# Up-projection products of 512 columns over both parts of the input, and the gate multiply on VectorE

## The chip, the cores and the metric

The kernel runs on one core of one Trainium2 chip. The metric is the device time in microseconds (us) of one execution. A core has five engines with queues of their own: TensorE (PE in the profile, its weight loads PEld), VectorE (DVE), ScalarE (ACT), GpSimd (POOL) and SyncE (SP, which here issues DMAs). They wait for each other by semaphores. TensorE writes its products into PSUM, eight banks of 512 float32 columns on 128 partitions; the other tiles lie in SBUF.

## The reference

A trunk of two transformer layers on 256 tokens of width 1024. Layer 0 has block-sparse attention, which at this length is plain causal attention, layer 1 has sliding-window attention with sinks. After each attention stands the channel mixer that the change touches:

```
def conv_ffn(h, w_up, conv_w, conv_b, w_down):
    S_ = h.shape[1]
    u = h @ w_up                                         # 1024 -> 2 * 2816
    up = jnp.pad(u, ((0, 0), (CONV_W - 1, 0), (0, 0)))
    u = conv_b + sum(conv_w[j] * up[:, j:j + S_] for j in range(CONV_W))
    gate, val = jnp.split(u, 2, axis=-1)
    return (jax.nn.silu(gate) * val) @ w_down

x = x + conv_ffn(rmsnorm(x, ffn_norm[l]), w_up[l], conv_w[l], conv_b[l], w_down[l])
```

All inputs and outputs are float32.

## The kernel before

**Split products.** Each float32 operand is split into a high part, rounded to the TensorE format float32r, and a low part, the remainder. A product is the sum of three: high by high, high by low and low by high. ScalarE rounds (`hi_part`, L177), VectorE subtracts (`lo_part`, L185).

**Weights.** All weights come as 90 units of 128 x 2048, 1 MB each. `fetch` (L166) issues the DMA on SP's queue into three raw buffers. `prepare(i)` splits a unit in two to eight pieces; its last step fetches unit i + 3. The high and the low parts have four buffers each. `used(i)` is called when the products of unit i have been issued, and lets unit i + 4 be prepared.

**Order of the work.** The program keeps a clock of its own: `tick` adds a planned time for each product issued on TensorE, and steps put off with `chain(key, (delay, step), ...)` are issued when the clock passes their due time. `require(key)` issues what is left of a chain at once. In the feed-forward part the scheduler of the framework may still move instructions within an engine's queue; each engine then runs its queue in order.

**The up-projection.** Per layer there are NF = 22 units; unit i holds for eight chunks c of the input the 128 gate columns (j = 0) and the 128 value columns (j = 1). The weights are the stationary operand, the 256 tokens the moving one. `mm` runs over j, then over the chunks: three products of 256 columns each (L683 high by high, L684 high weights by low input, L685 low weights by high input), 48 a unit. Gate and value land in the two halves of one PSUM bank. Units 0 to 3 (`i < n_raw`) read the input `hT` before its normalisation factor is known, and the factor is applied to their result; units 4 to 21 read `hS`, the scaled input, which `scale_x` splits into four pairs of chunks.

**After a unit, `post`.** ScalarE computes the last tap of the convolution with its bias (`tap2`, L718), VectorE adds the two others for gate and value (`taps`, L722 and L724), ScalarE applies SiLU (L728), GpSimd multiplies gate and value (L732), ScalarE rounds the result (L736), VectorE subtracts (L737). In units 4 to 21 `tap2` and `taps` read the PSUM bank itself. PSUM tags: "acc" has four banks, "t" and "u" two each; units 4 to 21 take one bank of "t" and "u" in turn.

**The down-projection, `Down`.** 11 weight units, each with two halves of 128 rows, two blocks of 128 tokens and products of 512 columns (L588, L589, L593), into the four "acc" banks. It needs the results of `post` for two up-projection units per weight unit.

The functions around the change:

Of the kernel before, what the change touches and what calls it, by code (L numbers as in the profile page):

```python
# [10 lines left out]
AF = mybir.ActivationFunctionType  # L11
ALU = mybir.AluOpType
AX = mybir.AxisListType

P = 128
D = 1024
S = 256
NB = S // P
KC = D // P
# [7 lines left out]
NF = DFF // P  # L27
# [32 lines left out]
def trunk(ctx: ExitStack, tc, x, xw, pos, cpk, fin, sinks, w, out):  # L60
    nc = tc.nc
# [8 lines left out]
    def nm(s):  # L70
        uid[0] += 1
        return f"{s}_{uid[0]}"
# [5 lines left out]
    def spaced(pool, n, dt, tag, name, bufs):  # L78
        return pool.tile([P, n + ROUND], dt, tag=tag, name=name, bufs=bufs)[:, SKIP:SKIP + n]

    def quad(dt=F32R, name="q"):
        return spaced(qd, 4 * S, dt, "q", nm(name), 15).rearrange("p (c t) -> p c t", c=4)

    def mid():
        return wk.tile([P, 512], F32, tag="m2", name=nm("m2"), bufs=6)

    def row3(n=3 * P):
        return wk.tile([P, 3 * P + 8], F32, tag="m3", name=nm("m3"), bufs=8)[:, 4:4 + n]
# [7 lines left out]
    def bank(tag):  # L96
        return ps.tile([P, 512], F32, tag=tag, name=nm(tag), bufs=4 if tag == "acc" else 2)

    def f(ap):
        return ap.bitcast(F32)  # L100
# [7 lines left out]
    def turns(ap):  # L108

        return ap.rearrange("p (a t) -> p t a", a=2)  # L110

    def pairs(ap):
        return ap.rearrange("p (t a) -> p t a", a=2)
# [8 lines left out]
    def run_item(item):  # L122
        put_off.remove(item)
        was, busy[0] = busy[0], True
        item[2]()
        busy[0] = was

    def tick(ns):
        clock[0] += ns
        while put_off and not busy[0]:  # L130
            item = min(put_off, key=lambda t: t[0])
            if item[0] > clock[0]:
                return
            run_item(item)

    def chain(key, *steps, urgent=0):

        def run(k):
            if urgent:
                with tc.high_priority(offset=urgent):  # L140
                    steps[k][1]()
            else:
                steps[k][1]()
            if k + 1 < len(steps):
                put_off.append((clock[0] + steps[k + 1][0], key, lambda: run(k + 1)))
        put_off.append((clock[0] + steps[0][0], key, lambda: run(0)))

    def require(*key):

        while True:  # L150
            mine = [t for t in put_off if t[1] == key]
            if not mine:
                return
            run_item(min(mine, key=lambda t: t[0]))


    wq = {}
# [55 lines left out]
    def used(i):  # L213

        prepare(i + 4)

    def need(i):
        require("w", i)
# [48 lines left out]
    for b in range(NB):  # L267
        t = one.tile([P, NH, HD], F32, name=f"v{b}")
# [12 lines left out]
    def new_hT():  # L281

        return [(quad(), quad()) for _ in range(2)]
# [71 lines left out]
    def hx(hT, c):  # L355
        hi, lo = hT[c // 4]
        return hi[:, c % 4], lo[:, c % 4]
# [306 lines left out]
    def ffn(layer, u_up, u_dn, hT, y, rb, after, tail=None):  # L664
        parts = []

        n_raw = 4
        hS = new_hT()

        def mm(i, up, cs_):  # L670
            need(u_up + i)
            hi, lo = wq[u_up + i]
            for j in range(2):
                o = up[j]
                for c in cs_:
                    if i < n_raw:
                        for b in range(NB):
                            require("x", b, c // 4)
                    else:
                        require("y", c // 2)  # L680
                    s_ = slice((2 * c + j) * P, (2 * c + j + 1) * P)
                    xh, xl = (turns(t) for t in hx(hT if i < n_raw else hS, c))
                    nc.tensor.matmul(pairs(o), hi[:, s_], xh, start=(c == 0), stop=False)  # L683
                    nc.tensor.matmul(pairs(o), hi[:, s_], xl, start=False, stop=False)  # L684
                    nc.tensor.matmul(pairs(o), lo[:, s_], xh, start=False, stop=(c == KC - 1))  # L685
                    tick(3 * 256 / 2.4)

        def scale_x(m):

            c = slice(2 * (m % 2), 2 * (m % 2) + 2)  # L690
            y_, hi, lo = (t[:, c] for t in (y[m // 2], *hS[m // 2]))

            def times():
                for b in range(NB):
                    require("rb", b)
                y4 = y_.rearrange("p c (a t) -> p c a t", a=2)
                r4 = rb.rearrange("p (t a) -> p a t", a=2).unsqueeze(1).to_broadcast([P, 2, 2, P])
                nc.vector.tensor_tensor(out=y4, in0=y4, in1=r4, op=ALU.mult)

            chain(("y", m), (2000.0 + 1000.0 * m, times), (700.0, lambda: nc.scalar.activation(hi, y_, AF.Copy)),  # L700
                  (600.0, lambda: nc.vector.tensor_tensor(out=lo, in0=y_, in1=f(hi), op=ALU.subtract)))

        def post(i, up, pq):
            hi, lo = pq[:, 2 * (i % 2)], pq[:, 2 * (i % 2) + 1]
            t = [row3(S) for _ in range(2)]
            gs, h = row3(S), row3(S)
            w0, w1, w2, bb = ([cp[:, CW + (layer * 2 * NF + j * NF + i) * 4 + k:][:, :1] for j in range(2)] for k in range(4))
            us = [mid()[:, :S] for _ in range(2)] if i < n_raw else up

            def scale():  # L710
                for b in range(NB):
                    require("rb", b)
                for j in range(2):
                    nc.vector.tensor_tensor(out=us[j], in0=up[j], in1=rb, op=ALU.mult)

            def tap2():
                for j in range(2):
                    nc.scalar.activation(t[j], us[j], AF.Identity, scale=w2[j], bias=bb[j])  # L718

            def taps():  # L720
                for j in range(2):
                    nc.vector.scalar_tensor_tensor(out=t[j][:, 1:], in0=us[j][:, :S - 1], scalar=w1[j], in1=t[j][:, 1:],  # L722
                                                   op0=ALU.mult, op1=ALU.add)
                    nc.vector.scalar_tensor_tensor(out=t[j][:, 2:], in0=us[j][:, :S - 2], scalar=w0[j], in1=t[j][:, 2:],  # L724
                                                   op0=ALU.mult, op1=ALU.add)

            def gate():
                nc.scalar.activation(gs, t[0], AF.Silu)  # L728
                if layer and i == NF - 1:

                    nc.scalar.activation(warm, gs[:, :1], AF.Sqrt, scale=0.0)
                nc.gpsimd.tensor_tensor(out=h, in0=gs, in1=t[1], op=ALU.mult)  # L732

            steps = [(200.0, scale), (700.0, tap2)] if i < n_raw else [(200.0, tap2)]
            chain(("p", i), *steps, (400.0, taps), (1600.0, gate),
                  (3400.0, lambda: nc.scalar.activation(hi, h, AF.Copy)),  # L736
                  (450.0, lambda: nc.vector.tensor_tensor(out=lo, in0=h, in1=f(hi), op=ALU.subtract)))  # L737
            parts.append((hi, lo))

        pq = quad()  # L740
        ups = [[bank(t)[:, :S] for _ in range(2)] for t in ("u", "acc")]
        for cs_ in (range(4), range(4, KC)):
            for i in range(2):
                mm(i, ups[i], cs_)
        for i in range(2):
            used(u_up + i)
            post(i, ups[i], pq)
        for m in range(4):
            scale_x(m)
        for i in range(2, NF):  # L750
            if i % 2 == 0:
                pq = quad()
            up = bank("acc" if i < 4 else "t" if i % 2 else "u")
            mm(i, [up[:, :S], up[:, S:]], range(KC))
            used(u_up + i)
            post(i, [up[:, :S], up[:, S:]], pq)

        def wait(i):
            require("p", 2 * i)
            require("p", 2 * i + 1)  # L760

        if tail is not None:
            nc.sync.dma_start(fin_t, fin.partition_broadcast(P))
        dn = Down(u_dn, NF // 2, parts, wait, tail is not None)
        for _ in dn.units(0, NF // 2 - 2):
            pass
        dn.finish(NF // 2 - 2, after, tail)
# [20 lines left out]
    hT = new_hT()  # L788
# [200 lines left out]
    hT = new_hT()  # L989
    y = [quad(F32, "y") for _ in range(2)]  # L990
# [13 lines left out]
    def after_f0(b, n):  # L1004
# [3 lines left out]
        raw_feats(b, n, xT_h, ("x", b, n))  # L1008

    ffn(0, U_UP0, U_DN0, hT, y, rb, after_f0)  # L1010


# [60 lines left out]
    hT = new_hT()  # L1073
    y = [quad(F32, "y") for _ in range(2)]
# [152 lines left out]
```

## Time and profile before

| | |
|---|---|
| time, median of 3 runs | 551.17 us (550.32 to 552.12) |
| profiled execution: time | 551.24 us |
| profiled execution: span from first to last instruction | 549.3 us |
| TensorE clock granted, mean | 0.998 |
| up-projection of layer 0, units 4 to 21 | about 136 to 233 us of the span |
| up-projection of layer 1, units 4 to 21 | about 389 to 486 us |
| GpSimd's 44 multiplies (L732) | 69.6 us busy, 1581 ns each on average |

In the rows below, a group reads: line, engine, operation, written tile <- read tiles, shapes, count, then busy time in us, mean ns of one, and idle time of the engine in front of them. Tile names: `wr` raw weights, `wh` and `wl` their high and low parts, `q` parts of activations, `m` intermediate rows in SBUF, `cp` the convolution's constants, and `acc`, `t`, `u` banks of PSUM.

A row of the busy time by windows reads: window, its length, then for each engine the busy time and the count of instructions, the granted clock, the DMA share and GB/s.

### The profile page before, as it was taken

How to read it: one execution, taken by the hardware profiler on the slowest of the kernel's cores; microseconds unless marked ns; L12 is line 12 of the kernel's file. 1: busy time of each engine (PE TensorE's matmuls, PEld its weight loads, DVE VectorE, ACT ScalarE, POOL GpSimd, SP SyncE). 2: the span in 40 equal slices, each digit the busy share in tenths (PEclk: the TensorE clock that was granted, in tenths of full speed). 3: DMA queues.
4: the chain of work that ended last, by engine and by line, in shares of the span. 5: the costliest groups of instructions: out<-in, count | busy, mean ns of one | idle time of the engine just before them, and what ended most of it. 6: DMA issues, size and time to landing. Idle time of an engine off the chain costs nothing.

```text
span 549.3 us, 9981 instructions
## 1 busy us (share of the span) xinstructions
PE 540.9 (98%) x3762; PEld 497.0 (90%) x3762; DVE 423.8 (77%) x901; ACT 373.3 (68%) x735; POOL 114.2 (21%) x155
## 2 busy tenths in 40 slices
PE   9999999999999999999999999999999999999995
PEld 7888888899999999988888887889999999998884
DVE  6798777589898888874468999878898898884514
ACT  6789778579577777754368888777657777683313
POOL 7312001011423332230000120102432332320003
PEclk9999999999999999999999999999999999999999
DMA  8975444432466556666552644242375656666201
GB/s 293 402 281 187 155 153 155 154 135 97 158 226 231 211 202 208 226 230 220 177 216 87 221 153 154 83 148 82 150 245 206 197 199 229 237 225 231 113 0 76
DMA packets 15311, 100.98 MB, mean 184 GB/s; under 512 B 1952, under 2 KB 2080, under 8 KB 3744
## 3 DMA queue, kind: packets, MB, share of 16 engines
q1 hardware_dynamic: 14976, 100.09, 50.5%
q8 instruction: 29, 0.48, 0.3%
q10 hardware_dynamic: 288, 0.26, 0.1%
q14 instruction: 18, 0.15, 0.1%
HBM read 99.30 MB, written 1.05 MB: 183 GB/s over the span
## 4 chain that ended last, share of the span: by engine, by line
PE 91%; ACT 3%; DMA 2%; DVE 2%; POOL 1%; issue 0%; ACTq 0%
PE acc L588 9%; PE acc L593 9%; PE acc L589 9%; PE u L683 7%; PE u L684 7%; PE u L685 6%; PE t L683 6%; PE t L684 6%; PE t L685 6%; PE acc L367 4%; PE acc L366 4%; PE acc L368 4%; PE acc L683 2%; PE acc L685 2%; PE acc L684 2%; PE t L538 2%
## 5 line engine op out<-in xcount | busy, mean ns | idle before, releaser
L185 DVE TENSOR_TENSOR wl<-wr,wh 128x1024 fp32r<-128x1024 f32 (+1 forms) x190 | 207.5, 1110 | 51.2 <-ACT wh L177 50.8
L177 ACT ACTIVATE wh<-wr 128x1024 fp32r<-128x1024 f32 (+1 forms) x188 | 175.1, 960 | 47.7 <-PE acc L593 41.5
L732 POOL TENSOR_TENSOR m<-m,m 128x256 f32<-128x256 f32 x44 | 69.6, 1581 | 168.5 <-DVE m L724 87.4
L588 PE MATMUL acc<-wh,q 128*128 128x512 f32 x238 | 92.2, 387 | 0.0
L589 PE MATMUL acc<-wl,q 128*128 128x512 f32 x238 | 90.5, 380 | 0.0
L683 PE MATMUL u<-q,wh 128*128 128x256 f32 x320 | 88.3, 277 | 0.0
L684 PE MATMUL u<-q,wh 128*128 128x256 f32 x320 | 88.1, 276 | 0.0
L685 PE MATMUL u<-q,wl 128*128 128x256 f32 x320 | 87.9, 275 | 0.0
L683 PE MATMUL t<-q,wh 128*128 128x256 f32 x288 | 79.2, 275 | 0.0
L684 PE MATMUL t<-q,wh 128*128 128x256 f32 x288 | 79.2, 275 | 0.0
L685 PE MATMUL t<-q,wl 128*128 128x256 f32 x288 | 79.2, 275 | 0.0
L593 PE MATMUL acc<-wh,q 128*128 128x512 f32 x238 | 74.5, 379 | 0.0
L685 PEld LDWEIGHTS u<-q,wl 128*128 128x128 f32 x320 | 61.4, 192 | 0.0
L684 PEld LDWEIGHTS u<-q,wh 128*128 128x128 f32 x320 | 61.4, 192 | 0.0
L683 PEld LDWEIGHTS u<-q,wh 128*128 128x128 f32 x320 | 61.3, 192 | 0.0
L683 PEld LDWEIGHTS t<-q,wh 128*128 128x128 f32 x288 | 55.3, 192 | 0.0
L684 PEld LDWEIGHTS t<-q,wh 128*128 128x128 f32 x288 | 55.3, 192 | 0.0
L685 PEld LDWEIGHTS t<-q,wl 128*128 128x128 f32 x288 | 55.3, 192 | 0.0
L588 PEld LDWEIGHTS acc<-wh,q 128*128 128x128 f32 x238 | 45.0, 189 | 6.7 <-issue 0.9
L593 PEld LDWEIGHTS acc<-wh,q 128*128 128x128 f32 x238 | 45.0, 189 | 6.3
L589 PEld LDWEIGHTS acc<-wl,q 128*128 128x128 f32 x238 | 45.0, 189 | 5.7
L736 ACT ACTIVATE q<-m 128x256 fp32r<-128x256 f32 x44 | 18.1, 416 | 46.4 <-POOL m L732 46.4
(179 smaller groups left out, 1031.3 us busy)
## 6 DMA issues: line engine op xcount, KB each, us to landing
wr<-in_w SPq DMA_DIRECT2D x90, 1024.0 KB, 4.8
first<-in_xw SPq DMA_DIRECT2D x5, 384.0 KB, 5.6
xr<-in_x SPq DMA_DIRECT2D x2, 512.0 KB, 9.9
first<-in_xw SPq DMA_DIRECT2D x1, 768.0 KB, 7.0
fin_t<-in_fin SPq DMA_DIRECT2D x1, 512.0 KB, 5.6
out<-ot SPq DMA_DIRECT2D x1, 512.0 KB, 2.6
first<-in_xw SPq DMA_DIRECT2D x1, 388.0 KB, 3.5
out<-m SPq DMA_DIRECT2D x1, 256.0 KB, 2.4
```

What stands on the lines that cost most here:

```text
L177: nc.scalar.activation(wq[i][0][:, c], raws[i][:, c], AF.Copy, **({} if g is None else {"scale": g}))
L185: nc.vector.tensor_tensor(out=wq[i][1][:, c], in0=raws[i][:, c], in1=f(wq[i][0][:, c]), op=ALU.subtract)
L366: nc.tensor.matmul(pairs(o), xh[:, blk(b)], turns(wh), start=(c == 0), stop=False)
L367: nc.tensor.matmul(pairs(o), xh[:, blk(b)], turns(wl), start=False, stop=False)
L368: nc.tensor.matmul(pairs(o), xl[:, blk(b)], turns(wh), start=False, stop=(c == KC - 1))
L588: nc.tensor.matmul(pairs(o), ph[:, blk(b)], turns(hi[:, s_]), start=first, stop=False)
L589: nc.tensor.matmul(pairs(o), ph[:, blk(b)], turns(lo[:, s_]), start=False, stop=False)
L593: nc.tensor.matmul(pairs(o), pl[:, blk(b)], turns(hi[:, s_]), start=False, stop=end)
L683: nc.tensor.matmul(pairs(o), hi[:, s_], xh, start=(c == 0), stop=False)
L684: nc.tensor.matmul(pairs(o), hi[:, s_], xl, start=False, stop=False)
L685: nc.tensor.matmul(pairs(o), lo[:, s_], xh, start=False, stop=(c == KC - 1))
L732: nc.gpsimd.tensor_tensor(out=h, in0=gs, in1=t[1], op=ALU.mult)
```

## The change

For units 4 to 21 the two parts of a chunk of the scaled input now lie next to each other in `hS`, and a new function `mm_scaled` multiplies the high weights with both in one product of 512 columns: high by high into columns 0 to 255 of a bank, high by low into columns 256 to 511. The low weights are multiplied with the high input as before, 256 columns, added onto columns 0 to 255. The chunks are the outer loop, gate and value the inner one. Gate and value have a PSUM bank each, taken from "u", "t" and "acc" in turn.

In `post` ScalarE copies columns 256 to 511 of each bank to SBUF (`aside`), VectorE adds columns 0 to 255 onto them (`both`), and `tap2` and `taps` read the sum in SBUF. The multiply of gate and value moves from GpSimd to VectorE, as a step of its own (`times`), in all 22 units; the delay ahead of the rounding becomes 600 instead of 3400.

```diff
-        hS = new_hT()
+        hS = [quad().rearrange("p c (k t) -> p (c k) t", k=1).rearrange("p (c k) t -> p c k t", k=2) for _ in range(KC // 2)]
+
+        def mm_scaled(i, up):
+            need(u_up + i)
+            hi, lo = wq[u_up + i]
+            for c in range(KC):
+                require("y", c // 2)
+                both = hS[c // 2][:, c % 2]
+                for j in range(2):
+                    s_ = slice((2 * c + j) * P, (2 * c + j + 1) * P)
+
+                    def high():
+                        nc.tensor.matmul(up[j].rearrange("p (k t a) -> p k t a", k=2, a=2), hi[:, s_],
+                                         both.rearrange("p k (a t) -> p k t a", a=2), start=(c == 0), stop=(c == KC - 1))
+
+                    def low():
+                        nc.tensor.matmul(pairs(up[j][:, :S]), lo[:, s_], turns(both[:, 0]), start=False, stop=False)
+
+                    for step in (low, high) if c == KC - 1 else (high, low):
+                        step()
+                    tick(3 * 256 / 2.4)
...
-            y_, hi, lo = (t[:, c] for t in (y[m // 2], *hS[m // 2]))
+            y_, hi, lo = y[m // 2][:, c], hS[m][:, :, 0], hS[m][:, :, 1]
...
-            us = [mid()[:, :S] for _ in range(2)] if i < n_raw else up
+            us = [t[:, j * S:(j + 1) * S] for t in (mid(),) for j in range(2)]
+
+            def aside():
+                for j in range(2):
+                    nc.scalar.activation(us[j], up[j][:, S:], AF.Copy)
+
+            def both():
+                for j in range(2):
+                    nc.vector.tensor_tensor(out=us[j], in0=up[j][:, :S], in1=us[j], op=ALU.add)
...
-                nc.gpsimd.tensor_tensor(out=h, in0=gs, in1=t[1], op=ALU.mult)
-
-            steps = [(200.0, scale), (700.0, tap2)] if i < n_raw else [(200.0, tap2)]
-            chain(("p", i), *steps, (400.0, taps), (1600.0, gate),
-                  (3400.0, lambda: nc.scalar.activation(hi, h, AF.Copy)),
+
+            def times():
+                nc.vector.tensor_tensor(out=h, in0=gs, in1=t[1], op=ALU.mult)
+
+            steps = [(200.0, scale), (700.0, tap2)] if i < n_raw else [(200.0, aside), (450.0, both), (700.0, tap2)]
+            chain(("p", i), *steps, (400.0, taps), (1600.0, gate), (600.0, times),
+                  (600.0, lambda: nc.scalar.activation(hi, h, AF.Copy)),
...
-            up = bank("acc" if i < 4 else "t" if i % 2 else "u")
-            mm(i, [up[:, :S], up[:, S:]], range(KC))
+            if i < n_raw:
+                up = bank("acc")
+                up = [up[:, :S], up[:, S:]]
+                mm(i, up, range(KC))
+            else:
+                up = [bank(("u", "t", "acc", "acc")[(NF - 1 - i) % 4]) for _ in range(2)]
+                mm_scaled(i, up)
             used(u_up + i)
-            post(i, [up[:, :S], up[:, S:]], pq)
+            post(i, up, pq)
```

More of the change, by code (lines that the diff above doesn't have):

```diff
@@ L675, in mm @@
                 for c in cs_:
[L676 to L680, printed above, removed]
+                    for b in range(NB):
+                        require("x", b, c // 4)
                     s_ = slice((2 * c + j) * P, (2 * c + j + 1) * P)
-                    xh, xl = (turns(t) for t in hx(hT if i < n_raw else hS, c))
+                    xh, xl = (turns(t) for t in hx(hT, c))
                     nc.tensor.matmul(pairs(o), hi[:, s_], xh, start=(c == 0), stop=False)
```

## The prediction

> **What bounds the kernel now.** I read the page's totals and chain first, then the stage where the changed products stand, then each engine's timeline in that stage. Times in the timelines are microseconds: start, duration, engine, line; a bracket is idle time before the row and what ended it.
>
> ```profile
> PE 540.9 (98%) x3762; PEld 497.0 (90%) x3762; DVE 423.8 (77%) x901; ACT 373.3 (68%) x735; POOL 114.2 (21%) x155
> PE 91%; ACT 3%; DMA 2%; DVE 2%; POOL 1%; issue 0%; ACTq 0%
> ```
>
> TensorE is busy 98% of the span and carries 91% of the chain that ended last. So only two things count: what the products themselves cost, and whether another engine starts to hold TensorE up. The next rows are from the busy time by windows (first row: products of L683 alone, from the first product of up-projection unit 4 to the last of unit 21; second: all engines), and two entries of the chain in the down-projection.
>
> ```profile
> 136.27:232.75 96.48, 79.20 (x288) 55.19 (x288) 1.00 0.58 208
> 170.00:200.00 30.00, 30.00 (x271) 30.00 (x270) 25.91 (x43) 21.93 (x36) 9.68 (x7) 1.00 0.59 212
> 240.25 0.43 PE acc L593 x2
> 279.11 0.43 PE acc L593 x2
> ```
>
> L683 issues one of three products of 256 columns, so 96.48 us hold 864 of them: 111.7 ns each, and 48 of them make a unit of 5.36 us. In the down-projection the chain repeats every six products of 512 columns; 30 such rounds lie between the two entries, 38.86 us / 180 = 215.9 ns each. Two products of 256 columns thus cost 223.4 ns, one of 512 costs 215.9. VectorE is busy 25.91 of 30 us beside this: near full. That is the second thing to price.
>
> **The change part by part.**
>
> *Products.* Per unit, 48 products of 256 columns become 16 of 512 and 16 of 256, with the same columns. Cost by rows: 16 x (215.9 + 111.7) = 5.24 us against 5.36, so 0.12 us saved per unit. It applies to units 4 to 21 of two layers: 36 x 0.12 = 4.3 us. All of it lies on the path, since TensorE never idles there. No row shows 512 and 256 columns in alternation. The nearest is a stretch where transposes of 128 columns interrupt products of 512, beside six transposes alone on the chain:
>
> ```profile
> 110.13 0.60 PE L294 MATMUL t<-ident,xr 128*128 128x128 f32 x4
> 110.48 0.46 PE L588 MATMUL acc<-wh,q 128*128 128x512 f32 x1
> 110.78 0.38 PE L589 MATMUL acc<-wl,q 128*128 128x512 f32 x1
> 98.91 0.65 PE u L515 x6
> ```
>
> Four transposes and one product take 110.78 - 110.13 = 0.65 us. Unmixed it would be 4 x 0.109 + 0.216 = 0.65, so mixing was free. Lower end for the short product: it falls to the 108.6 ns of a transpose, which seems to be what a product pays when it is limited by something other than its columns; that adds 16 x 3.1 ns x 36 = 1.8 us of gain, 6.1 in all. Upper end: the short product's excess passes to its neighbour as well and eats the saving of 7.5 ns a pair: no gain. A loss beyond that is excluded by the sum just made, 0.65 against 0.65. I take the middle, 4.3 us, because both of its prices are measured in long streams of this kernel. The Trainium skill, "TensorE: Matmul & The Clock Gate", section Back-to-back issue gap, gives N/2.4 + 2.5 ns for a product of N columns. By that rule a removed product saves only its 2.5 ns, 16 x 2.5 x 36 = 1.4 us in all; the trace agrees at 512 columns (215.8 by the rule, 215.9 here) and not at 256 (109.2 by the rule, 111.7 here), so the row decides.
>
> *Order of the chunks.* Chunk c is now the outer loop and the gate or value half j the inner one. The second half of a unit's weights and of the scaled input is first read after half a unit (2.6 us) instead of a quarter (1.3 us). That costs nothing and gives 1.3 us of slack.
>
> *VectorE.* One steady unit now, start to start:
>
> ```profile
> 169.28 1.21 DVE L185 TENSOR_TENSOR wl<-wr,wh 128x1024 fp32r<-128x1024 f32 x1
> 170.41 0.47 DVE L722 SCALAR_TENSOR_TENSOR m<-u,cp,m 128x255 f32<-128x255 f32 x1
> 171.56 0.42 DVE L737 TENSOR_TENSOR q<-m,q 128x256 fp32r<-128x256 f32 x1 [0.68 <-ACT q L736]
> 171.91 0.48 DVE L724 SCALAR_TENSOR_TENSOR m<-u,cp,m 128x254 f32<-128x254 f32 x1
> 172.30 0.47 DVE L722 SCALAR_TENSOR_TENSOR m<-u,cp,m 128x255 f32<-128x255 f32 x1
> 172.69 1.22 DVE L185 TENSOR_TENSOR wl<-wr,wh 128x1024 fp32r<-128x1024 f32 x1
> 173.82 0.48 DVE L724 SCALAR_TENSOR_TENSOR m<-u,cp,m 128x254 f32<-128x254 f32 x1
> 174.22 1.22 DVE L185 TENSOR_TENSOR wl<-wr,wh 128x1024 fp32r<-128x1024 f32 x1
> 133.47 0.75 DVE L714 TENSOR_TENSOR m<-acc,rb 128x256 f32<-128x256 f32 x2
> 134.14 0.68 DVE L701 TENSOR_TENSOR q<-y,q 128x512 fp32r<-128x512 f32 x1
> ```
>
> Durations overlap, so I take start to start: two L185 at 1.13, four taps at 0.39, L737 at 0.35: 4.18 us of work in a period of 4.94; most of the rest is the 0.68 wait. The two adds of halves read one PSUM and one SBUF operand of 256 columns, exactly the form of L714, of which two take 134.14 - 133.47 = 0.67. The multiply has the form of L737: 0.35. The taps now read SBUF, as those of each layer's first units do already:
>
> ```profile
> L722 DVE SCALAR_TENSOR_TENSOR m<-m,cp,m 128x255 f32<-128x255 f32 x16 | 7.3, 474 | 3.9 <-ACT m L718 3.9
> L724 DVE SCALAR_TENSOR_TENSOR m<-m,cp,m 128x254 f32<-128x254 f32 x16 | 8.2, 534 | 0.0
> 130.09 0.97 DVE L724 SCALAR_TENSOR_TENSOR m<-m,cp,m 128x254 f32<-128x254 f32 x1
> ```
>
> L722 lasts 474 ns from SBUF too; L724's mean of 534 is raised by a few near 0.97, so I take no change (at worst 2 x 0.06 = 0.12 us a unit). New work: 4.18 + 0.67 + 0.35 = 5.20 us per unit against 5.24 on TensorE. Without any wait VectorE just fits; each wait on top lets it fall behind.
>
> *What falling behind costs.* VectorE runs late, and has room to do so:
>
> ```profile
> 148.87 1.01 ACT L718 ACTIVATE m<-u,cp 128x256 f32<-128x256 f32 x2
> 228.44 1.00 ACT L718 ACTIVATE m<-u,cp 128x256 f32<-128x256 f32 x2
> 152.95 1.22 DVE L185 TENSOR_TENSOR wl<-wr,wh 128x1024 fp32r<-128x1024 f32 x1
> 144.54 0.48 DVE L722 SCALAR_TENSOR_TENSOR m<-m,cp,m 128x255 f32<-128x255 f32 x1 [1.96 <-ACT m L718]
> ```
>
> Unit 4's products end at 136.27 + 5.36 = 141.63, but its first step, L718, starts at 148.87, 7.2 us late; unit 20's starts 1.0 us late (228.44). The backlog is worked off at 5.36 - 4.94 = 0.42 us a unit. In the new kernel it is not worked off. TensorE feels it through the weights: counted back from the end of the stage, the L185 at 152.95 is the last half of unit 8, done at 154.17 and needed at 136.27 + 4 x 5.36 = 157.71. That margin of 3.5 us, plus 1.3 from the new order, is 4.8. Ahead of that point the new kernel adds four multiplies and unit 4's adds, 4 x 0.35 + 0.67 = 2.1 us, and loses the waits that came from GpSimd (1.96 in the row at 144.54), so the margin stands. Over the 14 units from 8 to 21 VectorE's period may be 5.24 + 4.8/14 = 5.58 us before TensorE waits, and 5.58 + 2.15/14 = 5.73 before the layer's gain of 2.15 us is gone.
>
> *Waits on VectorE.* Per unit there are now three hand-overs to ScalarE and back: halves added, scaled by ScalarE, taps; gate, multiply; multiply, rounded by ScalarE, subtract. Lower end: none is exposed, because weights, taps and adds of other units fill them. Upper end: each exposes a wait like the 0.68 in the row at 171.56, 2.0 us. I take 0.2 us, nearer the lower end, because of all the hand-overs in the steady rows only the one behind GpSimd shows a wait. VectorE's period is then 5.4, under 5.58: no cost to TensorE.
>
> *GpSimd.* Its multiply leaves:
>
> ```profile
> 169.53 1.55 POOL L732 TENSOR_TENSOR m<-m,m 128x256 f32<-128x256 f32 x1 [3.39 <-DVE m L724]
> 171.12 0.42 ACT L736 ACTIVATE q<-m 128x256 fp32r<-128x256 f32 x1 [1.30 <-POOL m L732]
> 412.54 0.73 POOL L732 TENSOR_TENSOR m<-m,m 128x256 f32<-128x256 f32 x1 [3.57 <-DVE m L724]
> 412.65 1.70 DVE L185 TENSOR_TENSOR wl<-wr,wh 128x1024 fp32r<-128x1024 f32 x1 [0.58 <-ACT wh L177]
> ```
>
> The 1.55 us are off the path, and the 1.30 that ScalarE waited behind them goes; next late there is VectorE's own queue. Where GpSimd got through in 0.73 us, VectorE's neighbouring split took 1.70 instead of 1.21, so the two slow each other. That also goes, a relief of 0.5 us in few units, counted at nothing. By the Trainium skill, "SBUF — State Buffer", section SBUF: two separate sides, the two share a port pair and the later one waits for the whole instruction; these two rows agree.
>
> *ScalarE.* Two more copies of 128x256 from PSUM, and L718 now reads SBUF:
>
> ```profile
> L336 ACT ACTIVATE q<-t 128x256 fp32r<-128x256 f32 x8 | 2.7, 374 | 0.8 <-PE t L330 0.7
> 134.13 1.08 ACT L718 ACTIVATE m<-m,cp 128x256 f32<-128x256 f32 x2
> ```
>
> At most 2 x 0.374 = 0.75, and L718 from SBUF takes 1.08 for two instead of 1.00. The window's 21.93 us of 30 at 4.94 a unit are 3.6 us, so 4.4 us a unit of 5.24. It fits; if it did not, the first halves of the weights would be late and VectorE with them.
>
> *Buffers and DMAs.* A unit now holds two PSUM banks, but all eight rotate and four units stay in flight, and a bank is free after the adds instead of after the taps. The last two "acc" units, 18 and 19, must be clear when the down-projection starts two units (10.5 us) after unit 19 ends; a lag near 8 us passes. No DMA is moved, and nothing passes SP's or GpSimd's queue. The weight fetch still hangs on the last L185 of a unit, three units (15.7 us) ahead of use, and lands in 4.8:
>
> ```profile
> wr<-in_w SPq DMA_DIRECT2D x90, 1024.0 KB, 4.8
> ```
>
> *Sum.* The profiled execution took 551.24 us, 1.9 over its span of 549.3 and 0.07 over the median of 551.17. 551.2 - 4.3 = 546.9 us, 0.8% faster. About 0.3%, 1.65 us, is what a measurement of this kernel can tell from no change.
>
> **The rivals.** *VectorE becomes the bound, slower.* Place: the three hand-overs in units 8 to 21. If two of them expose one ScalarE operation of 0.42 us each (L736's duration), the period is 5.20 + 0.84 = 6.04; TensorE then loses (6.04 - 5.58) x 14 = 6.4 us a layer, 12.9 in all, against a gain of 4.3: 559.8 us. It decides from 5.73 on. For it speaks the fit of 5.20 in 5.24, with queues in order on both engines; against it that 2.0 us of the old waits came from GpSimd and go.
>
> *The gain is eaten, no change.* A period of 5.7 gives 1.7 us a layer back: 546.9 + 3.4 = 550.3. The same result comes if the saving per pair is not there in alternation (the upper end above).
>
> *Larger gain.* The short product falls to 108.6 ns: 545.1 us. The drop of 111.7 to the transposes' price speaks for it, the long stream at 111.7 against it.
>
> **How the numbers follow.** The forecast, 546.9 with its own range 545.8 to 549.2: 0.47. Larger gain, 545.1: 0.09. Both are faster: 0.56. Gain eaten: 0.16. VectorE the bound: 0.28, half of it beyond its 559.8. The range from 544.9 to 560 leaves out that far half (0.14) and a little below.
>
> **What would show it.** After the change, starts of products in units 5 to 20 should repeat every 5.24 us, 327.6 ns a pair, with no idle time of TensorE. L185 and the new adds should lag the products by a steady 7 to 10 us instead of a shrinking lag. VectorE should be about 99% busy in the stage, GpSimd idle. Wrong would be: TensorE waiting on the low part of weights from about unit 12 on (VectorE the bound), or a pair of products over 335 ns without any wait (the price of alternation).

## The result, and the profile after

The changed kernel takes 547.0 us, median of 4 runs (546.86 to 547.52), beside 550.8 us of the kernel before (median of 4, 550.32 to 552.12): a ratio of 0.9929, 95% interval 0.9909 to 0.9948. That is 0.7% faster; 546.9 us was forecast. The medians are 3.8 us apart. The profiled execution took 546.86 us with a span of 545.1 us, 4.2 us shorter than the 549.3 of before; the forecast had 4.3.

The totals on the page of the changed kernel:

```profile
PE 537.0 (99%) x3186; PEld 478.4 (88%) x3186; DVE 456.7 (84%) x1017; ACT 393.2 (72%) x807; POOL 45.2 (8%) x111
```

TensorE has 576 instructions fewer and 3.9 us less busy time; VectorE has 33 us more, GpSimd 69 us less. Where the 4.2 us come from is seen in the busy time by windows: first the products of 512 columns alone (L685 is the high product now), from the first product of up-projection unit 4 to the start of the down-projection, then all engines in the middle of that stage.

```profile
136.41:230.74 94.33, 93.29 (x288) 53.08 (x288) 1.00 0.58 201
170.00:200.00 30.00, 30.00 (x185) 27.60 (x185) 30.00 (x59) 23.66 (x45) 0.00 (x0) 1.00 0.59 207
```

The 18 units take 94.33 us, 5.24 each, where they took 96.48: 2.15 us less in layer 0. In layer 1 they take 94.32 us (387.37 to 481.69), where they took 96.48 (389.43 to 485.91), so the two layers make 4.3. VectorE is busy for 30.00 of 30 us, GpSimd for nothing. TensorE's timeline shows the new rhythm:

```profile
136.41 0.38 PE L685 MATMUL t<-q,wh 128*128 128x512 f32 x1
136.63 0.27 PE L689 MATMUL t<-q,wl 128*128 128x256 f32 x1
136.74 0.38 PE L685 MATMUL t<-q,wh 128*128 128x512 f32 x1
...
140.67 0.38 PE L685 MATMUL t<-q,wh 128*128 128x512 f32 x1
```

From 136.41 to 140.67 lie 13 pairs: 327.7 ns a pair. The next product starts 0.22 us after one of 512 columns and 0.11 after one of 256, so each pays its own price, mixed or not. One unit on VectorE:

```profile
178.28 0.41 DVE L764 TENSOR_TENSOR m<-m,m 128x256 f32<-128x256 f32 x1
178.62 0.73 DVE L738 TENSOR_TENSOR m<-acc,m 128x256 f32<-128x256 f32 x2
179.28 0.40 DVE L769 TENSOR_TENSOR q<-m,q 128x256 fp32r<-128x256 f32 x1
179.62 1.21 DVE L185 TENSOR_TENSOR wl<-wr,wh 128x1024 fp32r<-128x1024 f32 x1
180.75 0.86 DVE L752 SCALAR_TENSOR_TENSOR m<-m,cp,m 128x255 f32<-128x255 f32 x2
181.54 0.86 DVE L754 SCALAR_TENSOR_TENSOR m<-m,cp,m 128x254 f32<-128x254 f32 x2
182.33 1.21 DVE L185 TENSOR_TENSOR wl<-wr,wh 128x1024 fp32r<-128x1024 f32 x1
183.47 0.41 DVE L764 TENSOR_TENSOR m<-m,m 128x256 f32<-128x256 f32 x1
183.80 0.74 DVE L738 TENSOR_TENSOR m<-acc,m 128x256 f32<-128x256 f32 x2
```

L738 are the adds of the halves, L764 is the multiply. From add to add 5.18 us pass, and no row has a bracket: not one wait in this unit. All of TensorE's waits in the changed kernel stand in this view of the waits (engine, line, releaser: sum in us, times, longest):

```profile
PE u L276 <- DVE warm L252: 1.1, 1, 1.1
PE t L409 <- DVE m L401: 0.4, 1, 0.4
PE acc L367 <- DVE wl L185: 0.2, 1, 0.2
PE acc L366 <- ACT wh L177: 0.2, 1, 0.2
```

None is in the up-projection or at the start of the down-projection.

### The profile page after: what moved, and what is told of

It reads as the page before. It is cut to its first block, busy times and chain, and to the rows that moved or that the text cites. A ratio compares the mean times of both kernels' runs of the same rounds, so it can differ in the third digit from the quotient of the medians.

```text
span 545.1 us, 8977 instructions
## 1 busy us (share of the span) xinstructions
PE 537.0 (99%) x3186; PEld 478.4 (88%) x3186; DVE 456.7 (84%) x1017; ACT 393.2 (72%) x807; POOL 45.2 (8%) x111
## 4 chain that ended last, share of the span: by engine, by line
PE 91%; ACT 3%; DMA 2%; DVE 2%; POOL 1%; issue 0%; ACTq 0%
PE acc L685 10%; PE acc L588 9%; PE acc L589 9%; PE acc L593 9%; PE t L685 6%; PE u L685 6%; PE acc L689 5%; PE acc L367 4%; PE acc L366 4%; PE acc L368 4%; PE u L689 3%; PE t L689 3%; PE acc L705 2%; PE acc L706 2%; PE acc L707 2%; PE t L538 2%
## 5 line engine op out<-in xcount | busy, mean ns | idle before, releaser
L588 PE MATMUL acc<-wh,q 128*128 128x512 f32 x238 | 92.2, 387 | 0.0
L589 PE MATMUL acc<-wl,q 128*128 128x512 f32 x238 | 90.5, 380 | 0.0
L685 PE MATMUL acc<-q,wh 128*128 128x512 f32 x256 | 84.2, 382 | 0.0
L593 PE MATMUL acc<-wh,q 128*128 128x512 f32 x238 | 74.5, 379 | 0.0
L689 PE MATMUL acc<-q,wl 128*128 128x256 f32 x256 | 67.2, 273 | 0.0
L748 ACT ACTIVATE m<-m,cp 128x256 f32<-128x256 f32 x88 | 49.3, 594 | 7.1 <-DVE m L738 4.3
L685 PE MATMUL t<-q,wh 128*128 128x512 f32 x160 | 53.5, 382 | 0.0
L685 PE MATMUL u<-q,wh 128*128 128x512 f32 x160 | 53.5, 382 | 0.0
L685 PEld LDWEIGHTS acc<-q,wh 128*128 128x128 f32 x256 | 47.8, 189 | 5.9
L689 PEld LDWEIGHTS acc<-q,wl 128*128 128x128 f32 x256 | 49.1, 192 | 0.8
L366 PE MATMUL acc<-wh,q 128*128 128x512 f32 x112 | 44.0, 393 | 0.2 <-ACT wh L177 0.2
L367 PE MATMUL acc<-wl,q 128*128 128x512 f32 x112 | 42.7, 381 | 0.2 <-DVE wl L185 0.2
L368 PE MATMUL acc<-wh,q 128*128 128x512 f32 x112 | 42.6, 380 | 0.0
L689 PE MATMUL u<-q,wl 128*128 128x256 f32 x160 | 42.0, 273 | 0.0
```

The costliest lines, as they stand in the source:

```text
L366: nc.tensor.matmul(pairs(o), xh[:, blk(b)], turns(wh), start=(c == 0), stop=False)
L367: nc.tensor.matmul(pairs(o), xh[:, blk(b)], turns(wl), start=False, stop=False)
L368: nc.tensor.matmul(pairs(o), xl[:, blk(b)], turns(wh), start=False, stop=(c == KC - 1))
L588: nc.tensor.matmul(pairs(o), ph[:, blk(b)], turns(hi[:, s_]), start=first, stop=False)
L589: nc.tensor.matmul(pairs(o), ph[:, blk(b)], turns(lo[:, s_]), start=False, stop=False)
L593: nc.tensor.matmul(pairs(o), pl[:, blk(b)], turns(hi[:, s_]), start=False, stop=end)
```

## The experiments

Times are medians; each ratio is to the kernel before on the same chip, with its 95% interval.

**The multiply back on GpSimd.** On the changed kernel, with a delay ahead of the rounding that fits the slower engine:

```diff
-                nc.vector.tensor_tensor(out=h, in0=gs, in1=t[1], op=ALU.mult)
+                nc.gpsimd.tensor_tensor(out=h, in0=gs, in1=t[1], op=ALU.mult)
...
-                  (600.0, lambda: nc.scalar.activation(hi, h, AF.Copy)),
+                  (2800.0, lambda: nc.scalar.activation(hi, h, AF.Copy)),
```

> The changed kernel with the multiply of gate and value back on GpSimd, due 600 after the SiLU, and the rounding 2800 after it. Theory (the products carry the whole gain, VectorE has room): the products stay as in the changed kernel, so 547 us, as long as the weights are still early enough. VectorE's work falls by 0.34 us a unit to 4.85, and the waits behind GpSimd come back (0.7 us a unit, as before the change), 5.5 in all, under the 5.58 that the prediction worked out: 547.0, at most 549. Rival (the move to VectorE was needed because the waits behind GpSimd eat the margin of the first units): TensorE waits for low parts of weights in units 6 to 10 of each layer, 549 to 553 us.

Measured: 554.65 us, ratio 1.0084 (1.0062 to 1.0107). Slower than before, and slower than either theory had it. The largest sum of TensorE's waits in this kernel, and then two rows of its timeline behind the start of the down-projection, which was at 230.08:

```profile
PE acc L588 <- DVE m L738: 4.7, 4, 1.3
```

```profile
232.63 0.48 PE L588 MATMUL acc<-wh,q 128*128 128x512 f32 x1 [1.09 <-DVE m L738]
234.62 0.48 PE L588 MATMUL acc<-wh,q 128*128 128x512 f32 x1 [1.28 <-DVE m L738]
```

TensorE does not wait for weights: it waits for the two "acc" banks of unit 19, which VectorE's late adds still hold. VectorE and GpSimd in a steady unit of this kernel:

```profile
189.24 0.42 DVE L738 TENSOR_TENSOR m<-acc,m 128x256 f32<-128x256 f32 x1
189.50 0.73 POOL L764 TENSOR_TENSOR m<-m,m 128x256 f32<-128x256 f32 x1 [4.72 <-ACT m L734]
189.57 1.73 DVE L185 TENSOR_TENSOR wl<-wr,wh 128x1024 fp32r<-128x1024 f32 x1
194.62 0.41 DVE L738 TENSOR_TENSOR m<-t,m 128x256 f32<-128x256 f32 x1
```

The period from add to add is 194.62 - 189.24 = 5.38 us, again with no idle time, though VectorE has the multiply less to do. The split that falls beside GpSimd's multiply takes 1.73 us instead of the 1.21 in the changed kernel. VectorE's own unit would be 5.18 - 0.34 = 4.84; with the 0.52 it is 5.36. In these units, then, giving the multiply away costs VectorE more than doing it.

Most of the lag, however, is older than that. The adds start 5.9 us after the end of unit 4's products and 11.7 us after the end of unit 12's; in the changed kernel these are 4.6 and 5.4. From 136 to 190 us VectorE is busy for 46.27 of 54 us, where it is busy for 53.99 in the changed kernel: it waits 7.7 us for steps of ScalarE, and ScalarE waits 10.7 us there for multiplies on GpSimd. One such chain:

```profile
156.47 2.67 POOL L764 TENSOR_TENSOR m<-m,m 128x256 f32<-128x256 f32 x1 [3.88 <-ACT m L758]
159.17 0.42 ACT L768 ACTIVATE q<-m 128x256 fp32r<-128x256 f32 x1 [2.50 <-POOL m L764]
159.89 0.42 DVE L738 TENSOR_TENSOR m<-acc,m 128x256 f32<-128x256 f32 x1 [1.01 <-ACT m L734]
```

ScalarE's rounding (L768) stands in its queue ahead of a copy of the next unit (L734), so VectorE's add, which needs the copy, waits for GpSimd too. The waits behind GpSimd that both theories named did come back, but what TensorE then waits for is the banks and not the weights.

**The multiply alone on VectorE.** The kernel before, with the moved multiply and its delays and nothing else:

```diff
-                nc.gpsimd.tensor_tensor(out=h, in0=gs, in1=t[1], op=ALU.mult)
+
+            def times():
+                nc.vector.tensor_tensor(out=h, in0=gs, in1=t[1], op=ALU.mult)
...
-            chain(("p", i), *steps, (400.0, taps), (1600.0, gate),
-                  (3400.0, lambda: nc.scalar.activation(hi, h, AF.Copy)),
+            chain(("p", i), *steps, (400.0, taps), (1600.0, gate), (600.0, times),
+                  (600.0, lambda: nc.scalar.activation(hi, h, AF.Copy)),
```

> The kernel before, with nothing changed but the multiply of gate and value moved from GpSimd to VectorE. Theory (TensorE's products set the time): 551.0 us, no change within 0.3%; the lag of the steps behind the products falls from 7 us at unit 4 to under 4. Rival (part of the gain came from GpSimd leaving VectorE's way): 549 to 550 us.

Measured: 551.1 us, ratio 1.0001 (0.9993 to 1.0010). By itself the move is worth nothing, so the gain is not the move's. The expected lag was missed: unit 4's products end at 136.12 + 5.36 = 141.48 here, and its first step on ScalarE starts at 146.85, 5.4 us later and not under 4 (7.2 before).

**One and two multiplies more on VectorE.** Each of units 4 to 21 gets one or two more multiplies of 128x256 in `both`, whose results are not used:

```diff
+                for _ in range(1):     # 2 in the second kernel
+                    nc.vector.tensor_tensor(out=h, in0=us[0], in1=us[1], op=ALU.mult)
```

> The changed kernel with one more VectorE multiply of 128x256 per unit in units 4 to 21, right behind the adds of the halves (its result is overwritten later). VectorE's period becomes 5.19 + 0.34 = 5.52 us a unit against 5.24 on TensorE. Theory (the weights are 3.7 us early at unit 8, and 1.3 us more by the order of the chunks): the backlog grows by 0.28 a unit, 3.9 us over 14 units, under 5.0: 547.0 us, no change. Rival (VectorE is full already, so what is added goes straight into the time): 18 x 0.28 x 2 = 10 us more, 557 us.

> The changed kernel with two more VectorE multiplies of 128x256 per unit in units 4 to 21. VectorE's period becomes 5.19 + 0.67 = 5.86 us. With one more, the adds of unit 19 came at 230.45, 0.6 us before the down-projection began at 231.06, and 5.0 us later than without. Theory (room for 4 to 6 us of backlog a layer, then TensorE waits at the start of the down-projection for the banks of units 18 and 19, or shortly before it for weights): the adds of unit 19 come at about 235.5 to 236.2, the second pair of banks is wanted at 232.2, so 4 us a layer: 555 us. Rival (the scheduler hides it in other idle time of VectorE): 547 to 549 us.

Measured: one more 547.04 us, ratio 0.9926 (0.9914 to 0.9938), no cost; two more 556.94 us, ratio 1.0101 (1.0088 to 1.0115), 9.9 us above the changed kernel. The adds of the kernel with two more, and what TensorE waits for in it:

```profile
189.15 0.75 DVE L738 TENSOR_TENSOR m<-acc,m 128x256 f32<-128x256 f32 x2
195.00 0.76 DVE L738 TENSOR_TENSOR m<-t,m 128x256 f32<-128x256 f32 x2
229.92 0.38 PE L689 MATMUL u<-q,wl 128*128 128x256 f32 x1 [0.34 <-DVE wl L185]
232.43 0.38 PE L588 MATMUL acc<-wh,q 128*128 128x512 f32 x1
236.54 0.45 PE L588 MATMUL acc<-wh,q 128*128 128x512 f32 x1 [2.65 <-DVE m L738]
491.38 0.77 PE L588 MATMUL acc<-wh,q 128*128 128x512 f32 x1 [2.65 <-DVE m L738]
```

VectorE's period is 5.85 us here and 5.52 with one more. The down-projection starts at 232.43 instead of 230.74. Of these 1.7 us, 0.7 are there before the stage, since unit 4 starts at 137.14 instead of 136.41. The other 0.96 us go to waits for the low part of weights in units 20 and 21, like the 0.34 at 229.92; in layer 1 the stage is as much longer (95.32 us). Then 2.65 us go to unit 19's banks, in both layers. In layer 1 some 1.6 us more go to a slower clock (last section). Together that is 9.5 of the 10.2 us by which the span grew.

**The order of products.** In the changed kernel, all 16 products of 512 columns of a unit first, then all 16 of 256, instead of in turn:

```diff
-                    def high():
...
-                    for step in (low, high) if c == KC - 1 else (high, low):
-                        step()
+                    nc.tensor.matmul(up[j].rearrange("p (k t a) -> p k t a", k=2, a=2), hi[:, piece(c, j)],
+                                     both.rearrange("p k (a t) -> p k t a", a=2), start=(c == 0), stop=False)
...
+            for c in range(KC):
+                both = hS[c // 2][:, c % 2]
+                for j in range(2):
+                    nc.tensor.matmul(pairs(up[j][:, :S]), lo[:, piece(c, j)], turns(both[:, 0]), start=False, stop=(c == KC - 1))
```

> The changed kernel with the products of a unit in another order: first the 16 of 512 columns, then the 16 of 256. Theory (each product has its price wherever it stands, 215.9 and 111.7 ns): the unit stays at 16 x 327.6 ns = 5.24 us and the time at 547.0. Rival (alternation has a price or a gain of its own): the sum of the two streams differs from 327.6 ns a pair; 5 ns a pair would be 16 x 36 x 5 ns = 2.9 us, so 544 or 550 us.

Measured: 547.54 us, ratio 0.9936 (0.9924 to 0.9948): as the changed kernel. Its timeline has the two prices unmixed:

```profile
176.48 1.95 PE L691 MATMUL acc<-q,wl 128*128 128x256 f32 x16
178.27 3.62 PE L685 MATMUL t<-q,wh 128*128 128x512 f32 x16
181.72 0.94 PE L691 MATMUL t<-q,wl 128*128 128x256 f32 x7
```

Start to start, 16 of 256 take 1.79 us and 16 of 512 take 3.45: 111.9 and 215.6 ns, 327.5 together, where the alternation has 327.7.

**Where the multiply matters.** In the changed kernel, GpSimd multiplies either in units 4 to 21 alone (`i >= n_raw`, called late here) or in units 0 to 3 alone (`i < n_raw`, called early):

```diff
-                nc.vector.tensor_tensor(out=h, in0=gs, in1=t[1], op=ALU.mult)
+                (nc.gpsimd if i >= n_raw else nc.vector).tensor_tensor(out=h, in0=gs, in1=t[1], op=ALU.mult)
...
-                  (600.0, lambda: nc.scalar.activation(hi, h, AF.Copy)),
+                  (2800.0 if i >= n_raw else 600.0, lambda: nc.scalar.activation(hi, h, AF.Copy)),
```

> The changed kernel with the multiply on VectorE in units 0 to 3 and on GpSimd in units 4 to 21. Theory (GpSimd's multiply costs through VectorE's period: each one makes a split of weights next to it last 1.73 instead of 1.21 us, so that the period is 5.37 us, more than TensorE's 5.24, and the backlog never shrinks): the adds of unit 19 come late at the start of the down-projection, 550 to 555 us. Rival (only the backlog at the start counts, from the multiplies of units 0 to 3, which take up to 4.95 us on GpSimd): 547 to 548 us.

> The changed kernel with the multiply on GpSimd in units 0 to 3 and on VectorE in units 4 to 21. Theory (the period in units 4 to 21 decides; there it is 5.19): the backlog at unit 4 grows by some 2 us from waits behind GpSimd and stays under the room of 5 us: 547 us. Rival (the backlog at the start decides): 550 to 555 us.

Measured: late 546.5 us, ratio 0.9914 (0.9900 to 0.9927); early 547.11 us, ratio 0.9918 (0.9904 to 0.9931). The theory that the longer period of units 4 to 21 decides has fallen: with that period and no backlog from units 0 to 3 nothing is lost. Nor does GpSimd in units 0 to 3 alone cost anything, though more than a backlog comes with it: VectorE's period there is 5.18 us in units 9 to 12, but about 5.58 from unit 13 on, with waits on ScalarE's high part of weights. VectorE's last adds of units 18 and 19 in early, then that of unit 19 in the kernel with all multiplies on GpSimd; the adds of unit 19 clear the second bank that the down-projection needs:

```profile
227.12 0.42 DVE L738 TENSOR_TENSOR m<-acc,m 128x256 f32<-128x256 f32 x1
232.69 0.42 DVE L738 TENSOR_TENSOR m<-acc,m 128x256 f32<-128x256 f32 x1
```

```profile
234.15 0.41 DVE L738 TENSOR_TENSOR m<-acc,m 128x256 f32<-128x256 f32 x1
```

That bank is wanted by the second block of tokens, eight products of 215.9 ns = 1.7 us after the down-projection's start. All six kernels in one table (starts from the timelines, us):

| kernel | adds of unit 12 | second bank free | wanted | time |
|---|---|---|---|---|
| changed | 188.98 | 227.9 | 232.4 | 547.0 |
| GpSimd in units 4 to 21 | 189.66 | 229.6 | 232.2 | 546.5 |
| one multiply more | 191.50 | 231.2 | 232.8 | 547.04 |
| GpSimd in units 0 to 3 | 192.16 | 233.1 | 233.2 | 547.11 |
| GpSimd in all units | 194.62 | 234.6 | 231.8 | 554.65 |
| two multiplies more | 195.00 | 236.7 | 234.1 | 556.94 |

The time is flat until the bank comes free after it is wanted, and then it jumps: in the last two rows the bank is 2.8 and 2.6 us late, in each of two layers. GpSimd in units 0 to 3 stops just short of it. A backlog from the start, waits on the way and a longer period are all paid from the same 4.5 us of room. Either half of GpSimd's multiplies leaves some of it (VectorE waits 2.4 us in early and 2.2 in late from 136 to 190 us), both halves together overdraw it (7.7 us), and two multiplies more overdraw it by the period alone.

**The merged products in units 0 to 3 too.** The unscaled input `hT` gets the layout of `hS`, and units 0 to 3 run `mm_scaled` with `aside`, `both` and then `scale`:

```diff
-                both = hS[c // 2][:, c % 2]
+                both = (hT if i < n_raw else hS)[c // 2][:, c % 2]
...
-            steps = [(200.0, scale), (700.0, tap2)] if i < n_raw else [(200.0, aside), (450.0, both), (700.0, tap2)]
+            steps = [(200.0, aside), (450.0, both)] + ([(450.0, scale)] if i < n_raw else []) + [(700.0, tap2)]
...
-                mm(i, ups[i], cs_)
+                mm_scaled(i, ups[i], cs_)
```

> The changed kernel with products of 512 columns in units 0 to 3 as well: their input is laid out in the same way, their halves are copied and added like those of the others, and the factor is applied to the sum. Theory (0.12 us a unit, whichever unit it is): 8 x 0.12 = 1.0 us less, 546.0 us. VectorE has 4 x 0.67 = 2.7 us more to do early in each layer, where weights are 3.6 us early, so TensorE need not wait. Rival (the early margin is used up, or a wait for the banks of unit 1 comes in): 547 to 550 us.

Measured: 546.95 us, ratio 0.9921 (0.9908 to 0.9935): no gain over the changed kernel. TensorE's timeline in this kernel, from the last product ahead of the stage:

```profile
113.10 0.38 PE L597 MATMUL acc<-wh,q 128*128 128x512 f32 x1
114.32 0.48 PE L690 MATMUL u<-q,wh 128*128 128x512 f32 x1 [0.28 <-DVE q L320]
136.47 0.38 PE L690 MATMUL t<-q,wh 128*128 128x512 f32 x1
```

The same place in the changed kernel:

```profile
113.05 0.38 PE L593 MATMUL acc<-wh,q 128*128 128x512 f32 x1
113.74 0.38 PE L705 MATMUL u<-q,wh 128*128 128x256 f32 x1
```

A merged product needs the low part of the input, which VectorE makes last (L320). So the up-projection starts 1.22 us after the last product ahead of it instead of 0.69: 0.53 us later, against the 64 x 7.5 ns = 0.48 us that merging saves in these units. Unit 4 starts at 136.47 where it started at 136.41.

**All merged but the start.** As the last kernel, but the first four chunks of units 0 and 1 keep three products of 256 columns, so that the first needs only the high part:

```diff
+                    if i < 2 and c < 4:
+                        nc.tensor.matmul(pairs(up[j][:, :S]), hi[:, s_], turns(both[:, 0]), start=(c == 0), stop=False)
+                        nc.tensor.matmul(pairs(up[j][:, S:]), hi[:, s_], turns(both[:, 1]), start=False, stop=False)
+                        low()
+                        tick(3 * 256 / 2.4)
+                        continue
```

> Products of 512 columns in units 0 to 3 too, but in units 0 and 1 the first four chunks stay in three products of 256, so that the first product of the stage need not wait for the low part of its input. Theory (the missing gain of the run with all units was the 0.5 us a layer by which its first product started later): 2 x (24 x 2 + 8 x 2... ) counted in merged pairs, 48 a layer of the 64, 48 x 2 x 7.5 ns = 0.7 us less than the changed kernel, 546.3. Rival (the copies and adds of the early units make it wait elsewhere): 547.0 or more.

Measured: 545.82 us, ratio 0.9910 (0.9896 to 0.9923), the fastest of all; its interval overlaps that of the changed kernel, so the time alone does not separate them. From the last product ahead of the stage to unit 4 in its timeline:

```profile
112.62 0.38 PE L597 MATMUL acc<-wh,q 128*128 128x512 f32 x1
135.72 0.38 PE L690 MATMUL t<-q,wh 128*128 128x512 f32 x1
```

23.10 us, where the changed kernel has 136.41 - 113.05 = 23.36: 0.26 us saved a layer, where 48 x 7.5 ns = 0.36 were to be had. What is left of the wait ahead of the start was not pursued.

**The price per product by itself.** In the changed kernel, 666 of the 714 products of 512 columns of the down- and output projections are split into two of 256:

```diff
-            for n, c in cols:
-                o = self.acc[b][n][:, c]
...
+                    for m in range(0, 2, w):
+                        yield (pairs(self.acc[b][n][:, m * S:(m + w) * S]),
+                               *(turns(t[:, s_])[:, m * P:(m + w) * P] for t in (hi, lo)), m + w == 2)
```

> The changed kernel with the products of 512 columns in the down and output projections (L588, L589, L593) split into two of 256 each, except the first three of each bank: 666 of the 714 are split, with the same columns and the same order of weights. Theory (a product more costs 7.5 ns whatever it belongs to, 2 x 111.7 - 215.9): 666 x 7.5 = 5.0 us more, 552.0. Rival (a product more costs only 2.5 ns, the rule of the Trainium skill, TensorE: Matmul & The Clock Gate, section Back-to-back issue gap): 666 x 2.5 = 1.7 us more, 548.7.

Measured: 551.7 us, ratio 1.0013 (1.0004 to 1.0022): 4.7 us above the changed kernel, 7.1 ns for each of the 666 products added. Its timeline:

```profile
250.10 0.28 PE L594 MATMUL acc<-wh,q 128*128 128x256 f32 x1
...
251.44 0.28 PE L594 MATMUL acc<-wh,q 128*128 128x256 f32 x1
```

Twelve products lie between these two rows: 1.34 us / 12 = 111.7 ns, in another stage with other operands.

What the 7.5 ns belong to stays open. Every product in these kernels comes with a weight load of its own (3186 of each in the changed kernel, 3852 in this one), so each edit moves both. Where all products have 256 columns the weight loads leave no gap: PEld is busy for 30.00 of 30 us from 250 to 280 us here, as it was from 170 to 200 us before the change, against 27.60 in the changed kernel's stage. That the short product is held up by weight loads fits this, and no run separates the two.

## Why the prediction was right

*Products: right.* 5.24 us a unit and 4.3 us in all were forecast, and 5.24 and 4.2 (by the spans) measured; a pair was to take 327.6 ns and takes 327.7. That alternation is free (the choice between the upper and the lower end) was shown by the kernel with the products in two streams. That the saving is a price for each product (with its weight load), about 7.5 ns, was shown a second time by splitting products elsewhere. By the 2.5 ns of the Trainium skill, "TensorE: Matmul & The Clock Gate", section Back-to-back issue gap, that split would have cost 1.7 us where it cost 4.7; the section gives them for a product by itself and says that weight loads add to them at few columns. The rows, not that rule, gave the gain.

*Order of chunks: free, as said.* No wait for weights appeared; no run changed the order alone.

*VectorE's work: right.* 5.20 us a unit forecast, 5.18 measured. *Its waits: mis-sized, harmlessly.* 0.2 us were taken, none is there in units 8 to 16; the upper end of 2.0 was far off. From unit 18 on, however, the adds follow every 5.58 us with the same work, so some 0.4 us a unit are waits, half of which shows in front of a split of weights:

```profile
226.38 1.23 DVE L185 TENSOR_TENSOR wl<-wr,wh 128x1024 fp32r<-128x1024 f32 x1 [0.18 <-ACT wh L177]
```

Why they begin there was not tested.

*The backlog: mis-sized.* "7.2 us late" at unit 4 was carried over from before. In the changed kernel unit 4's first step and its adds:

```profile
142.89 0.63 ACT L734 ACTIVATE m<-t 128x256 f32<-128x256 f32 x2
146.29 0.74 DVE L738 TENSOR_TENSOR m<-t,m 128x256 f32<-128x256 f32 x2
```

Unit 4 ends at 136.41 + 5.24 = 141.65, so these are 1.2 and 4.6 us late. Later the adds lag by 5.4 to 5.6 us in units 8 to 12, steady as said, but not 7 to 10. The 7.2 us were read at the convolution's last tap, which now comes after the copy and the add; in the changed kernel it (L748) starts at 147.12, 5.5 us late. So the fall is 1.7 us. The step that was mis-sized is that the multiplies in units 0 to 3 were counted as 0.35 us of new work each, against one wait of 1.96 us that goes, with nothing left over. The move alone took the lag from 7.2 to 5.4 us, and with GpSimd back in those four units alone the tap is 7.6 us late and the adds 6.9 (unit 4 ends at 142.45 there): GpSimd's part of the backlog was about 2 us, the larger part was not GpSimd's.

*The margin of the weights: right.* 3.5 us early was forecast for unit 8. The last low half of unit 8 in the changed kernel, and the first product of unit 8:

```profile
152.47 1.22 DVE L185 TENSOR_TENSOR wl<-wr,wh 128x1024 fp32r<-128x1024 f32 x1
157.38 0.38 PE L685 MATMUL t<-q,wh 128*128 128x512 f32 x1
```

Done at 153.69, 3.7 us early. *The point from which TensorE was to wait: too low.* The prediction's 5.58 us counts the margin to the start of unit 8 and adds 1.3. But this last half of the weights is first read half a unit later, at 157.38 + 2.62 = 160.00, so the margin is 6.3 us and not 4.8; and from unit 8 to unit 21 there are 13 steps, not 14. That gives 5.24 + 6.3/13 = 5.73 us. Periods of 5.52 and, for the last nine units of one kernel, 5.58 were free; at 5.85 TensorE waits for low weights.

*What gives way first: missed.* The prediction sized the rival "VectorE becomes the bound" by the weights, and let the banks of units 18 and 19 off with "a lag near 8 us passes". In both kernels in which VectorE ran late enough to matter, the banks of unit 19 cost the most: 4.7 us of waits in the one, 5.3 us in the other. The rival's formula gives 2 x 14 x (5.85 - 5.58) = 7.6 us for two multiplies more. 9.9 were measured, of which only 1.9 are waits for weights.

*GpSimd: a term left out.* The relief was "counted at nothing". In the merged kernel, from unit 11 on, the multiply on GpSimd costs VectorE 0.52 us a unit, more than the 0.34 of doing it there, and before that VectorE waits behind it. So the products carry the gain, but with all multiplies on GpSimd the kernel is slower than before: the prediction priced the move only as a burden on the new products, and it also makes room for them. Half of the move would have been enough: with GpSimd in units 0 to 3 or in units 4 to 21 alone nothing is lost.

*ScalarE and DMAs: as said.* ScalarE is busy 23.66 of 30 us, 4.1 a unit (4.4 forecast); the two copies take 0.63 (at most 0.75 forecast).

## What to carry to other kernels

Take the price of an instruction from long streams of your own trace at both sizes: a difference of 7.5 ns in 111.7 was the whole result, and it came out to 0.1 us. Before you hand work to an idle engine to relieve a busy one, look at what its neighbour's instructions take while it runs, and at what waits in a third engine's queue behind its result. For an engine that runs late by a steady amount, list every deadline it serves (weights, banks, the next stage's first product) and find the nearest; until that one was crossed here lateness cost nothing, and beyond it TensorE lost what the engine was late by, in every layer.

## What was not expected of the hardware

*The clock.* After the wait of 2.65 us in layer 1 of the kernel with two multiplies more, the granted clock (the column after the five engines) fell; after the same wait in layer 0 it did not. The windows of both:

```profile
491.00:494.50 3.50, 3.12 (x8) 2.52 (x9) 3.50 (x9) 2.46 (x6) 0.00 (x0) 0.55 0.77 269
236.00:240.00 4.00, 3.46 (x16) 3.09 (x17) 4.00 (x11) 2.47 (x6) 0.00 (x0) 1.00 0.74 262
```

A mean of 0.55 over 3.5 us is half clock for 3.15 us of it, so 1.6 us are lost on top of the wait. The kernel with GpSimd in all units shows 0.50 in layer 1 after its waits of 1.0 and 1.3 us, and not in layer 0. The Trainium skill, "TensorE: Matmul & The Clock Gate", section What's actually happening, has a clock of half or full, set by the activity in free-running windows of about 3.4 us; that fits a wait that sometimes costs a window and sometimes not. It lets the clock fall after an idle window of that length, and here 2.65 us of waiting were enough. Where the windows lay is not seen in these runs.

*The shared port.* GpSimd's multiply runs for 0.73 us and holds VectorE's split up by 0.52. The Trainium skill, "SBUF — State Buffer", section SBUF: two separate sides, describes an exclusive lock between a GpSimd instruction and a VectorE one with two SBUF inputs; the rows at 189.50 and 189.57 agree. From 189 us on one split of every unit was hit in this way; why always the one was not tested.
